# A gated four-branch decoder layer on one core: seven-product halves for 19 groups of column blocks in place of 7, with weight tiles placed by the form of the product

## Chip, cores and metric

The kernel runs on one core of a Trainium2 chip. The metric is the device time of one execution in microseconds (us). Every time below is from a run or from the profiled execution of the kernel before.

## What is computed

One layer, 256 tokens of width 2048, and 256 memory tokens, all in float32:

```python
xn = rms_norm(x, ln_g)
(a_q, a_k, a_v, a_g, c_b, c_c, c_h, c_g, s_q, s_k, s_v, s_g, m_q, m_g,      # 14 sections of 1024 columns
 i_q, i_k, i_w,                                                             # 324 columns of an indexer
 r_a, r_c, r_s, r_m) = [xn @ w for w in cols]                               # 4 gates of 2048 columns
y_a = moba_attention(a_q, a_k, a_v) * silu(a_g)                             # one block of 256: causal
y_c = c_b * short_conv(c_c * c_h, conv_w, conv_b) * silu(c_g)               # depthwise, width 3
y_s = dsa_attention(s_q, s_k, s_v, i_q, i_k, i_w) * silu(s_g)               # top 64 keys of each token
mk, mv = split(rms_norm(mem, mem_ln_g) @ w_mem_kv)
y_m = memory_attention(m_q, mk, mv) * silu(m_g)
merged = (sigmoid(r_a) * (y_a @ w_branch[0]) + sigmoid(r_c) * (y_c @ w_branch[1])
          + sigmoid(r_s) * (y_s @ w_branch[2]) + sigmoid(r_m) * (y_m @ w_branch[3]))
out = rms_norm(x + merged @ w_out, final_g)
```

## The kernel before

**Split products.** Each float32 operand is split into a high part (rounded by ScalarE, line 104) and a low part (the rest, by VectorE, line 105), and a product is three matmuls: high by high, high by low, low by high. Weights come from HBM in tiles `raw` of 1 MB (four buffers), and each is split in two steps of 128x1024 into `hi` and `lo` (four buffers each). So every weight costs ScalarE a cast and VectorE a subtraction beside TensorE's matmuls.

**Two forms.** In the form with tokens moving (`project_t`, `products_t`, lines 135 to 151) the weight block is stationary and 256 token columns move; the result stands with channels on partitions, as the attention wants it. A section of 1024 columns is 384 matmuls of 256 columns. In the form with weights moving (`project`, `products`, lines 157 to 177) a block of 128 tokens is stationary and 512 weight columns move; the result has tokens on partitions. Two blocks of 512 columns are 192 matmuls of 512 columns, which streams as many columns as the other form does.

**Seven-product halves.** `by_halves` (lines 222 to 270) takes two blocks of 512 columns, "a group" below. On the first 1024 rows of the weights it forms a two by two product (two blocks of tokens, two quarters of 512 rows, two column blocks) with seven products in place of eight; the other 1024 rows go through in plain form (`plain`). A group is 180 matmuls of 512 columns in place of 192. For it, sums of blocks of the activations are made once (`sums_of`, into `x_sums`), and sums of weight quarters each time: four subtractions of 128x2048 in place in `raw` (lines 241, 245, 251, 261). The quarters `b11`, `b12` and `b22` hold three of the four `raw` buffers for most of the group. The products pass through the banks `m`, `z`, `r`, `x`, `y`, and eight additions of 128x512 put them together (lines 248 to 269). Where weights are plain, VectorE makes 16 splits for two blocks; in a group it makes 22, since the products use sums as well.

**Where which form stands.** Token-moving: the sections for q, k and gates (`to_heads`, `to_gate`), the convolution's four, the indexer, and the memory's k. Weights moving and plain: the memory's v, the first of two halves (j = 0) of the gate columns of M, S and A, the branch projections `w` and the output. By halves: the v sections of S and A, the second gate halves of M, S and A, and both gate halves of C, seven groups. `finish` (line 584) makes the SiLU gate, then for each j the gate columns and `merge`, which multiplies the branch projection `w` by the gate and adds it up.

**Order.** The order of each engine's queue is made by a scheduler from the program's order and its own estimates; each engine then works its queue in that order. TensorE runs M, S, A and C in turn, with the attention's small matmuls set between the matmuls of the next projection.

Of the kernel before, what the change touches and what calls it, by code (L numbers as in the profile page):

```python
# [36 lines left out]
SECTIONS_T = [(c, W) for c in (M_Q, M_G, S_Q, S_K, S_G, A_Q, A_K, A_G, C_C, C_H, C_B, C_G)]  # L37
SECTIONS_N = [(S_V, W), (A_V, W), (R_0, 4 * D)]
# [6 lines left out]
TOPK = 64  # L45


@with_exitstack
def hybrid_kernel(ctx, tc, x, xT, mem, memT, ln_g, mem_ln_g, w_t, w_n, w_idx, conv_w, conv_b, w_mem_k, w_mem_v,
# [26 lines left out]
    cb = const.tile([P, 8], F32, name="cb")  # L76
    nc.gpsimd.dma_start(out=g_x, in_=ln_g)
# [255 lines left out]

    def to_gate(c0, val):

        y = big.tile([P, 8, 2, T], F32R, name="y", tag="y")
        for b in range(4):
            cs = slice(2 * b, 2 * b + 2)
            yt = tmp.tile([P, 2, T], F32, name="yt", tag="yt")
            copy_t(yt, project_t(w_t[FIRST[c0] + b], x_act), func=AF.Silu)  # L340
            nc.vector.tensor_mul(yt, yt, val[:, cs])
            split(y[:, cs, 0], y[:, cs, 1], yt)
# [161 lines left out]
    def first_columns(dst):  # L504
# [4 lines left out]
        for k0 in range(0, KC, 4):  # L509
            raw = raw_tile(NB).rearrange("p k (b c) -> p k b c", b=2)  # L510
            n = 1 if k0 == 0 else 2
            for k in range(k0, k0 + 4, n):
# [3 lines left out]
                for i in range(n):  # L516
                    if (k + i) % 2 == 0:
                        hi, lo = parts_tiles(NB, NB)
# [65 lines left out]
    def finish(b, gate, val, halved, after=None):  # L584

        y = to_gate(gate, val)
        for j in range(2):
            merge(b, j, gate_columns(b, j, halved[j]), y, after)

    finish(BR_M, M_G, q, (False, True))  # L590
# [7 lines left out]
    finish(BR_S, S_G, q, (False, True))  # L598
# [22 lines left out]
    for b in range(4):  # L621
        acc = project_t(w_t[FIRST[C_B] + b], x_act)
        for j in range(2):
            nc.vector.tensor_mul(cc[:, 2 * b + j], acc[j], cc[:, 2 * b + j])
# [11 lines left out]
    finish(BR_C, C_G, cc, (True, True), after=parts_of)  # L636
# [4 lines left out]
    junk = big.tile([P, 2, NB], F32, name="junk", tag="nat")  # L641
# [9 lines left out]
    for n, (c0, c) in enumerate(blocks):  # L651
        ns = slice(c0, c0 + c)
        acc = project(w_out[c0 // NB][:, :, c0 % NB:c0 % NB + c], lambda k: mt[:, k], "o", t_outer=(n == last))
        for t in range(2):
            o = xr[t][:, ns]
            nc.vector.tensor_add(o, acc[t], o)
            nc.scalar.activation(out=junk[:, t, :c], in_=o, func=AF.Square, accum_out=ss[:, t, n:n + 1])
            if n < last:
                nc.vector.tensor_mul(o, o, fg[:, ns])
            if n == last - 1:  # L660
                nc.vector.tensor_reduce(out=pre[:, t:t + 1], in_=ss[:, t, :last], axis=AX.X, op=ALU.add)
                nc.vector.tensor_scalar(pre[:, t:t + 1], pre[:, t:t + 1], 1.0 / D, EPS, op0=ALU.mult, op1=ALU.add)
            if n == last:
# [50 lines left out]
```

## Time and profile before

| | |
|---|---|
| three runs | 1397.42, 1400.25 (median), 1401.28 us |
| the profiled execution | 1398.06 us; span of its profile 1396.3 us |
| TensorE matmuls, weight loads | 99% and 89% of the span busy, 8796 of each |
| VectorE, ScalarE, GpSimd | 67%, 52%, 1% |
| mean DMA rate | 193 GB/s |

TensorE's matmuls are pipelined: the mean of one in the profile (some 390 ns for 512 columns) is longer than the distance from one start to the next. The distance is found from a stretch that holds one kind alone: its length and one duration more, over the count, since the count takes in what lies partly in the stretch. On VectorE too an instruction overlaps the next by some 80 ns, so a row of several is shorter than the sum of its durations.

### The profile page before, as it was taken

What the parts mean: (1) busy time and instruction counts of PE and PEld (TensorE: products, weight loads), DVE (VectorE), ACT (ScalarE), POOL (GpSimd) and SP (SyncE); (2) the same over time, 40 slices, a digit from 0 to 9 for tenths busy, and PEclk for the clock granted to TensorE, in tenths of its full rate; (3) what the DMA queues carried; (4) which work ended last, traced back from release to release, by engine and by line L of the source; (5) the groups of instructions that cost most, each with busy time, mean ns of one, the idle gap of its engine ahead of it and who ended that gap; (6) DMA issues with size and microseconds to landing.
All of it is one profiled execution on the core that took longest, in us unless ns stands there. A gap on an engine that the chain in (4) does not pass through costs nothing.

```text
span 1396.3 us, 21263 instructions
## 1 busy us (share of the span) xinstructions
PE 1380.4 (99%) x8796; PEld 1243.9 (89%) x8796; DVE 933.4 (67%) x1123; ACT 729.2 (52%) x991; POOL 11.0 (1%) x25
## 2 busy tenths in 40 slices
PE   9999999999999999999999999999999999999997
PEld 9998998789998898878999899878999998878887
DVE  7687764774848884596546885487547558787654
ACT  7663675453445684354445585445343345545443
POOL 1000000000000000000000000000000000000000
PEclk9999999999999999999999999999999999999999
DMA  9774545375554735537553746537555654736551
GB/s 343 291 271 173 191 156 180 128 266 189 172 197 133 254 128 183 189 135 247 188 193 133 243 150 211 182 125 266 183 181 187 225 192 148 265 130 241 183 197 73
DMA packets 49969, 269.49 MB, mean 193 GB/s; under 512 B 6656, under 2 KB 17456, under 8 KB 19024
## 3 DMA queue, kind: packets, MB, share of 16 engines
q1 hardware_dynamic: 48960, 264.03, 55.0%
q0 software_dynamic: 624, 3.31, 0.6%
q8 instruction: 69, 1.13, 0.3%
q10 hardware_dynamic: 288, 0.79, 0.1%
q14 instruction: 28, 0.23, 0.0%
HBM read 265.88 MB, written 2.10 MB: 192 GB/s over the span
## 4 chain that ended last, share of the span: by engine, by line
PE 85%; DVE 8%; DMA 3%; issue 2%; ACT 2%; SPq 0%; POOLq 0%; POOL 0%; DVEq 0%; ACTq 0%
PE acc L138 13%; PE acc L140 13%; PE acc L139 13%; DVE lo L105 5%; PE w L160 4%; PE w L161 4%; PE w L159 4%; PE r L159 4%; PE r L161 4%; PE r L160 4%; PE o L160 2%; PE o L161 2%; PE o L159 2%; DMA raw<-in_w_n 1%; PE y L160 1%
## 5 line engine op out<-in xcount | busy, mean ns | idle before, releaser
L105 DVE TENSOR_TENSOR lo<-raw,hi 128x1024 fp32r<-128x1024 f32 (+1 forms) x538 | 640.0, 1202 | 416.5 <-ACT hi L104 414.4
L104 ACT CAST hi<-raw 128x1024 fp32r<-128x1024 f32 (+1 forms) x538 | 552.2, 1032 | 547.8 <-PE acc L139 196.4
L139 PE MATMUL acc<-x_hl,hi 128*128 128x256 f32 x1520 | 426.0, 280 | 0.0
L138 PE MATMUL acc<-x_hl,hi 128*128 128x256 f32 x1520 | 425.4, 280 | 0.5 <-ACT qt L155 0.5
L140 PE MATMUL acc<-x_hl,lo 128*128 128x256 f32 x1520 | 425.8, 280 | 0.0
L140 PEld LDWEIGHTS acc<-x_hl,lo 128*128 128x128 f32 x1520 | 288.1, 190 | 0.1
L138 PEld LDWEIGHTS acc<-x_hl,hi 128*128 128x128 f32 x1520 | 284.8, 187 | 0.9 <-ACT qt L155 0.7
L139 PEld LDWEIGHTS acc<-x_hl,hi 128*128 128x128 f32 x1520 | 284.8, 187 | 0.2
L159 PE MATMUL w<-hi,y 128*128 128x512 f32 x256 | 99.9, 390 | 0.0
L161 PE MATMUL w<-hi,y 128*128 128x512 f32 x256 | 99.7, 389 | 0.0
L160 PE MATMUL w<-lo,y 128*128 128x512 f32 x256 | 99.6, 389 | 0.0
L159 PE MATMUL r<-hi,x_hl 128*128 128x512 f32 x248 | 98.3, 396 | 0.0
L161 PE MATMUL r<-hi,x_hl 128*128 128x512 f32 x248 | 97.9, 395 | 0.0
L160 PE MATMUL r<-lo,x_hl 128*128 128x512 f32 x248 | 97.6, 394 | 0.0
L159 PEld LDWEIGHTS w<-hi,y 128*128 128x128 f32 x256 | 48.1, 188 | 10.0
L161 PEld LDWEIGHTS w<-hi,y 128*128 128x128 f32 x256 | 48.1, 188 | 10.0
L160 PEld LDWEIGHTS w<-lo,y 128*128 128x128 f32 x256 | 48.1, 188 | 9.9
L161 PEld LDWEIGHTS r<-hi,x_hl 128*128 128x128 f32 x248 | 46.7, 188 | 10.6
L160 PEld LDWEIGHTS r<-lo,x_hl 128*128 128x128 f32 x248 | 46.7, 188 | 10.4
L159 PEld LDWEIGHTS r<-hi,x_hl 128*128 128x128 f32 x248 | 46.9, 189 | 10.2
L161 PE MATMUL o<-hi,mt 128*128 128x512 f32 (+1 forms) x160 | 55.3, 347 | 0.0
L160 PE MATMUL o<-lo,mt 128*128 128x512 f32 (+1 forms) x160 | 55.1, 346 | 0.0
(246 smaller groups left out, 1860.7 us busy)
## 6 DMA issues: line engine op xcount, KB each, us to landing
raw<-in_w_t SPq DMA_DIRECT2D x92, 1024.0 KB, 5.0
raw<-in_w_n SPq DMA_DIRECT2D x80, 1024.0 KB, 4.9
raw<-in_w_branch SPq DMA_DIRECT2D x32, 1024.0 KB, 5.3
raw<-in_w_out SPq DMA_DIRECT2D x16, 1024.0 KB, 4.8
raw<-in_w_mem_k SPq DMA_DIRECT2D x8, 1024.0 KB, 6.4
raw<-in_w_mem_v SPq DMA_DIRECT2D x8, 1024.0 KB, 5.5
raw<-in_w_t SPq DMA_DIRECT2D x16, 256.0 KB, 5.9
raw<-in_memT SPq DMA_DIRECT2D x2, 1024.0 KB, 8.8
```

Of the source, the lines that this page charges most:

```text
L104: nc.scalar.copy(out=hi, in_=src)
L105: nc.vector.tensor_sub(out=lo, in0=src, in1=hi.bitcast(F32))
L138: nc.tensor.matmul(o, lhsT=hi, rhs=a[:, 0], start=(k == 0), stop=False)
L139: nc.tensor.matmul(o, lhsT=hi, rhs=a[:, 1], start=False, stop=False)
L140: nc.tensor.matmul(o, lhsT=lo, rhs=a[:, 0], start=False, stop=(k == nk - 1))
L159: nc.tensor.matmul(o, lhsT=ah, rhs=hi, start=start, stop=False)
L160: nc.tensor.matmul(o, lhsT=ah, rhs=lo, start=False, stop=False)
L161: nc.tensor.matmul(o, lhsT=al, rhs=hi, start=False, stop=stop)
```

## The change

1. **Halves for twelve more groups.** The sections for q and k of S and A and the four of the convolution go from the token-moving form to groups of halves (eight groups); the first gate halves of M, S and A go from plain to halves (three); the first two blocks of the output go by halves, with sums of the merged activations, `m_sums` (one). 19 groups in all.
2. **Transposes.** q and k come out with tokens on partitions, so `transposed` turns them with 16 transposes of 128x128 on TensorE for a section, in four banks that ScalarE copies. In the convolution the products `c_c * c_h` and `silu(c_g) * c_b` are formed with tokens on partitions (`times`: four multiplications of 128x512 on VectorE) and each is turned once: six times 16 transposes. The convolution itself, 24 operations of 128x256 on VectorE, is as before, and now stands beside the group for `c_g`.
3. **Placement.** A `fill` of 224 bytes, `hi` and `lo` tiles of 2\*512+64 columns and a wider `u` set where tiles start. Before, `x_hl`, `mt` and the sums start 32 bytes past a multiple of 128, and `y`, `hi`, `lo` and `part` 96 bytes past one: in the weights-moving form `x_hl` and `hi` are 64 bytes apart, `y` and `hi` 0. After, all start at multiples of 128, but for `hi` and `lo` where 256-column weight blocks are used, which start 64 bytes past one (`place`): weights moving is 0 apart for `x_hl`, `mt`, the sums and `y`, tokens moving 64 apart, as before.
4. `yt` has one buffer in place of two; `junk` stands in the buffer of `y`.

The TensorE instructions go from 8796 to 7212: the matmuls of 512 columns from 3084 to 4476, those of 256 columns in split form from 5520 to 2448, the transposes from 102 to 198.

```diff
-SECTIONS_T = [(c, W) for c in (M_Q, M_G, S_Q, S_K, S_G, A_Q, A_K, A_G, C_C, C_H, C_B, C_G)]
-SECTIONS_N = [(S_V, W), (A_V, W), (R_0, 4 * D)]
+SECTIONS_T = [(c, W) for c in (M_Q, M_G, S_G, A_G)]
+SECTIONS_N = [(c, W) for c in (S_Q, S_K, S_V, A_Q, A_K, A_V, C_C, C_H, C_G, C_B)] + [(R_0, 4 * D)]
+STATIONARY = 64
+    fill = const.tile([P, 56], F32, name="fill")
...
+    def parts_tiles(w=NB, c=NB, place=0):
+        i = place // 4
+        return [spl.tile([P, 2 * NB + 64], F32R, name=n, tag=n)[:, i:i + 2 * NB]
+                .rearrange("p (k c) -> p k c", c=w)[:, :, :c] for n in ("hi", "lo")]
...
-                hi, lo = parts_tiles(w, c)
+                hi, lo = parts_tiles(w, c, STATIONARY if w == TB else 0)
...
+    def times(nat, dst):
+        def done(t, n, src, psum):
+            nc.vector.tensor_mul(part(dst, t, n), src, part(dst, t, n))
+        return done
+    def transposed(nat, done):
+        for c in range(0, 8, 2):
+            pp = halves(bank("tp", "s"))
+            for i in range(2):
+                for t in range(2):
+                    nc.tensor.transpose(pp[:, i, t * P:(t + 1) * P], nat[:, t, (c + i) * P:(c + i + 1) * P], ident)
+            done(c, pp)
     def to_heads(name, c0):
         dst = big.tile([P, 8, T], F32, name=name, tag=name)
-        for b in range(4):
-            copy_t(dst[:, 2 * b:2 * b + 2], project_t(w_t[FIRST[c0] + b], x_act))
+        nat = nat_tile("n" + name)
+        columns(c0, nat, kept(nat), True)
+        transposed(nat, lambda c, pp: nc.scalar.copy(out=dst[:, c:c + 2], in_=pp))
...
+    def finish(b, y, after=None, last=None):
         for j in range(2):
-            merge(b, j, gate_columns(b, j, halved[j]), y, after)
+            sig = gate_columns(b, j, True)
+            if j == 1 and last is not None:
+                last()
+            merge(b, j, sig, y, after)
...
-    cc = to_heads("qt", C_C)
+    uu = nat_tile("uu", "vv")
+    columns(C_C, uu, kept(uu), True)
+    nat = nat_tile("ch")
+    columns(C_H, nat, times(nat, uu), True)
...
+    transposed(uu, lambda c, pp: nc.scalar.copy(out=u[:, c:c + 2, 2:], in_=pp))
...
+    bg = nat_tile("bg", "vv")
+    columns(C_G, bg, through(bg, AF.Silu), True)
+    nat = nat_tile("cb")
+    columns(C_B, nat, times(nat, bg), True)
+    y = y_parts()
+    transposed(bg, lambda c, pp: gate_parts(y, yt_tile(), pp, cc, c))
...
+    finish(BR_C, y, after=parts_of, last=merged_sums)
+    sums_of(lambda k0, n: mt[:, k0:k0 + n], m_sums[0])
...
+        by_halves([w_out[0], w_out[1]], lambda k: mt[:, k], m_sums[0], nat,
+                  lambda t, n, src, psum: got.append((n, t, src)))
```

How the engines' queues change at three places. First TensorE at the seam between q and k of branch A (k begins here). Before, in the token-moving form, with `acc` the result, `x_hl` moving and `hi` or `lo` stationary:

```order
L138 MATMUL acc_6864<-x_hl_113,hi_6868 128x256
L139 MATMUL acc_6864<-x_hl_113,hi_6868 128x256
L140 MATMUL acc_6864<-x_hl_113,lo_6869 128x256
L138 MATMUL acc_6865<-x_hl_113,hi_6868 128x256
L139 MATMUL acc_6865<-x_hl_113,hi_6868 128x256
L140 MATMUL acc_6865<-x_hl_113,lo_6869 128x256
L138 MATMUL acc_6864<-x_hl_113,hi_6868 128x256
```

After, the end of the first product `m` of k's group, then q's transposes `tp`, then the plain part `z`:

```order
L166 MATMUL m<-hi,x_hl 128x512
L167 MATMUL m<-lo,x_hl 128x512
L168 MATMUL m<-hi,x_hl 128x512
L340 MATMUL tp<-ident,nqt 128x128 x2
L166 MATMUL z<-hi,x_hl 128x512
L167 MATMUL z<-lo,x_hl 128x512
L168 MATMUL z<-hi,x_hl 128x512
```

Behind the first product of 12 matmuls stand the first two transposes of q; `z` stands behind them. Next VectorE where the convolution stands (`u` its input, `cw` its weights, `lo<-raw,hi` the split of the next weights). Before, its operations for two column blocks stand between the splits of a token-moving section:

```order
L614 TENSOR_TENSOR u<-acc,qt 128x256 x2
L617 TENSOR_SCALAR qt<-u,cw,cb 128x256 x2
L619 SCALAR_TENSOR_TENSOR qt<-u,cw,qt 128x256
L105 TENSOR_TENSOR lo<-raw,hi 128x1024
L619 SCALAR_TENSOR_TENSOR qt<-u,cw,qt 128x256 x3
L105 TENSOR_TENSOR lo<-raw,hi 128x1024 x3
L614 TENSOR_TENSOR u<-acc,qt 128x256 x2
L617 TENSOR_SCALAR qt<-u,cw,cb 128x256 x2
L619 SCALAR_TENSOR_TENSOR qt<-u,cw,qt 128x256
```

After, in the group for `c_g`, with `cc` the convolution's result:

```order
L653 SCALAR_TENSOR_TENSOR cc<-u,cw,cc 128x256 x2
L110 TENSOR_TENSOR lo<-raw,hi 128x1024 x2
L653 SCALAR_TENSOR_TENSOR cc<-u,cw,cc 128x256
L651 TENSOR_SCALAR cc<-u,cw,cb 128x256
L653 SCALAR_TENSOR_TENSOR cc<-u,cw,cc 128x256
L651 TENSOR_SCALAR cc<-u,cw,cb 128x256 x5
L653 SCALAR_TENSOR_TENSOR cc<-u,cw,cc 128x256 x9
L268 TENSOR_TENSOR raw<-raw 128x2048
L653 SCALAR_TENSOR_TENSOR cc<-u,cw,cc 128x256
L110 TENSOR_TENSOR lo<-raw,hi 128x1024
L653 SCALAR_TENSOR_TENSOR cc<-u,cw,cc 128x256 x2
L110 TENSOR_TENSOR lo<-raw,hi 128x1024
```

18 operations of the convolution and a subtraction of weight quarters now stand between one split and the next. Last, VectorE in S's q section after the change, where the indexer's top-k (`MAX`, `MATCH_REPLACE` on `score`) stands between the group's own instructions:

```order
L110 TENSOR_TENSOR lo<-raw,hi 128x1024
L500 MAX m_3393<-score 128x8
L256 TENSOR_TENSOR nqt<-m,nqt 128x512
L110 TENSOR_TENSOR lo<-raw,hi 128x1024
L501 MATCH_REPLACE score<-m_3393,score 128x128
L268 TENSOR_TENSOR raw<-raw 128x2048
L110 TENSOR_TENSOR lo<-raw,hi 128x1024
L500 MAX m_3393<-score 128x8
L261 TENSOR_TENSOR nqt<-m,nqt 128x512
L262 TENSOR_TENSOR nqt<-m,nqt 128x512
```

Before, these rounds stood between the splits of the token-moving q section, with no `raw<-raw` and no `nqt` among them.

## Rows read from the trace of the kernel before

**Rows 1.** The page of the kernel before, its first part (busy time, share of the span, instructions), and from its fourth part (the chain of work that ended last) the line by engine.

```profile
PE 1380.4 (99%) x8796; PEld 1243.9 (89%) x8796; DVE 933.4 (67%) x1123; ACT 729.2 (52%) x991; POOL 11.0 (1%) x25
PE 85%; DVE 8%; DMA 3%; issue 2%; ACT 2%; SPq 0%; POOLq 0%; POOL 0%; DVEq 0%; ACTq 0%
```

**Rows 2.** Busy time by stretch (the windows view). Columns: the stretch in us and its length; for each engine its busy time and, in brackets, the instructions that lie at least partly in it; the granted share of the clock; the DMA engines' share; GB/s. In order: the q, k and v sections of branch S; S's earlier gate half; the k section of branch A; A's later gate half; the two gate halves of branch C; the first two column blocks of the output.

```profile
342.70:389.40 46.70, 46.70 (x405) 46.49 (x404) 36.08 (x79) 20.99 (x29) 1.10 (x2) 1.00 0.58 197
389.40:432.90 43.50, 43.50 (x387) 43.50 (x386) 21.75 (x18) 19.34 (x26) 0.00 (x0) 1.00 0.52 180
432.90:476.00 43.10, 42.88 (x194) 35.02 (x193) 38.29 (x40) 26.52 (x32) 0.00 (x0) 1.00 0.60 208
531.90:576.70 44.80, 44.80 (x195) 36.29 (x194) 20.83 (x18) 20.49 (x23) 0.00 (x0) 1.00 0.55 182
710.60:755.80 45.20, 45.20 (x386) 45.20 (x385) 21.93 (x18) 19.25 (x26) 0.00 (x0) 1.00 0.50 171
921.40:965.30 43.90, 42.27 (x182) 33.50 (x181) 38.80 (x37) 23.99 (x25) 0.00 (x0) 1.00 0.59 203
1168.00:1210.40 42.40, 42.06 (x183) 33.47 (x182) 37.33 (x35) 26.08 (x29) 0.53 (x1) 1.00 0.67 236
1233.10:1276.40 43.30, 42.36 (x182) 33.40 (x181) 38.14 (x36) 23.98 (x25) 0.00 (x0) 1.00 0.60 208
1299.90:1344.80 44.90, 44.90 (x202) 36.90 (x202) 25.61 (x27) 19.14 (x22) 0.00 (x0) 1.00 0.51 178
```

**Rows 3.** The same view inside stretches that hold one kind of product alone: `acc` of S's q and k sections; `acc` of the convolution's sections; `r` of S's earlier gate half; `w` of branch A; `r` of M's earlier gate half.

```profile
360.00:430.00 70.00, 70.00 (x620) 70.00 (x619) 44.38 (x78) 30.54 (x39) 0.00 (x0) 1.00 0.57 195
990.00:1160.00 170.00, 170.00 (x1446) 170.00 (x1445) 91.72 (x106) 69.47 (x78) 0.54 (x1) 1.00 0.56 192
534.00:574.00 40.00, 40.00 (x173) 32.42 (x172) 18.69 (x17) 17.49 (x18) 0.00 (x0) 1.00 0.55 185
901.00:921.00 20.00, 20.00 (x90) 16.58 (x89) 13.40 (x13) 7.73 (x8) 0.00 (x0) 1.00 0.46 157
221.00:237.00 16.00, 16.00 (x71) 13.13 (x70) 7.53 (x7) 5.88 (x7) 0.00 (x0) 1.00 0.60 198
```

**Rows 4.** VectorE's instructions in the later gate half of branch A, 921.4 to 965.3 us, grouped by line and shape (busy us, mean ns of one | idle before, and on what).

```profile
L105 DVE TENSOR_TENSOR lo<-raw,hi 128x1024 fp32r<-128x1024 f32 x23 | 27.2, 1219 | 4.8 <-ACT hi L104 4.8
L245 DVE TENSOR_TENSOR raw<-raw 128x2048 f32<-128x2048 f32 x1 | 2.3, 2284 | 0.0
L248 DVE TENSOR_TENSOR sig<-m,sig 128x512 f32<-128x512 f32 x1 | 0.7, 684 | 0.0
```

**Rows 5.** VectorE's timeline in the same stretch: start, length of the row, line, operands, count, and idle time before it with what ended it.

```profile
942.84 2.29 DVE L261 TENSOR_TENSOR raw<-raw 128x2048 f32<-128x2048 f32 x1 [0.29 <-DMA raw<-in_w_n]
946.18 0.68 DVE L254 TENSOR_TENSOR sig<-m,sig 128x512 f32<-128x512 f32 x1
946.78 0.68 DVE L255 TENSOR_TENSOR sig<-m,sig 128x512 f32<-128x512 f32 x1
951.98 5.76 DVE L105 TENSOR_TENSOR lo<-raw,hi 128x1024 fp32r<-128x1024 f32 x5
```

**Rows 6.** The chain that ended last, followed through the same stretch (start us, us, what).

```profile
929.92 2.21 DVE raw L245
932.24 1.05 ACT hi L104
933.31 0.98 DVE lo L105
934.46 3.50 DVE lo L105 x3
937.97 4.84 DMA raw<-in_w_n
942.84 1.21 DVE raw L261
...
953.25 0.50 PE y L160
```

**Rows 7.** All waits of TensorE (the waits view): who waited for whom, us in total, times, longest; its rows on `m` and `y`.

```profile
PE m L160 <- DVE lo L105: 3.3, 5, 0.8
PE m L159 <- ACT hi L104: 1.6, 2, 0.8
PE y L160 <- DVE lo L105: 0.4, 2, 0.2
```

**Rows 8.** TensorE's timeline where branch C's merged columns are transposed: the eight transposes, and the product behind them.

```profile
1227.41 1.04 PE L633 MATMUL pp<-ident,merged 128*128 128x128 f32 x8
1228.21 0.48 PE L159 MATMUL w<-hi,y 128*128 128x512 f32 x1
```

**Rows 9.** VectorE's groups, by line and shape: the convolution's operations on its eight column blocks (two lines); the indexer's top-k, its eight rounds on the full width, in S's q section (two lines); the split of one sum of the activations.

```profile
L617 DVE TENSOR_SCALAR qt<-u,cw,cb 128x256 f32<-128x256 f32 x8 | 2.9, 406 | 0.0
L619 DVE SCALAR_TENSOR_TENSOR qt<-u,cw,qt 128x256 f32<-128x256 f32 x16 | 7.0, 478 | 0.0
L469 DVE MAX8 m<-score 128x8 f32<-128x256 f32 x8 | 3.4, 426 | 0.2
L470 DVE MATCH_REPLACE8 score<-m,score 128x256 f32<-128x256 f32 x8 | 3.3, 409 | 0.0
L105 DVE TENSOR_TENSOR x_sums<-g,x_sums 128x512 fp32r<-128x512 f32 x4 | 2.6, 683 | 0.0
```

More of the change, by code (lines that the diff above doesn't have):

```diff
@@ L517, in first_columns @@
                     if (k + i) % 2 == 0:
[L518 removed]
+                        hi, lo = parts_tiles(place=STATIONARY)
                     split_tokens(xraw[:, k + i], k + i, g_x, x_hl[:, k + i])
@@ L620, in hybrid_kernel @@
                                            op0=ALU.mult, op1=ALU.add)
[L621 to L624, printed above, removed]
+    bg = nat_tile("bg", "vv")
+    columns(C_G, bg, through(bg, AF.Silu), True)
+    nat = nat_tile("cb")
+    columns(C_B, nat, times(nat, bg), True)
+    y = y_parts()
+    transposed(bg, lambda c, pp: gate_parts(y, yt_tile(), pp, cc, c))
     mt = big.tile([P, KC, 2, T], F32R, name="mt", tag="xhl")
@@ L650, in hybrid_kernel @@
     inv = const.tile([P, 2], F32, name="o_inv")
-    for n, (c0, c) in enumerate(blocks):
-        ns = slice(c0, c0 + c)
[L653 to L663, printed above, removed]
-                nc.vector.tensor_scalar(var[:, t:t + 1], ss[:, t, n:], 1.0 / D, pre[:, t:t + 1], op0=ALU.mult,
-                                        op1=ALU.add)
-                nc.gpsimd.tensor_tensor(out=inv[:, t:t + 1], in0=var[:, t:t + 1], in1=mhalf[:, 0:1], op=ALU.pow)
-                nc.vector.tensor_mul(o, o, fg[:, ns])
-                for eng, cs in ((nc.vector, slice(0, 512)), (nc.scalar, slice(512, 1280)), (nc.vector, slice(1280, D))):
-                    o = xr[t][:, cs]
-                    if eng is nc.vector:
-                        nc.vector.tensor_scalar(o, o, inv[:, t:t + 1], None, op0=ALU.mult)
-                    else:
-                        nc.scalar.activation(out=o, in_=o, func=AF.Copy, scale=inv[:, t:t + 1])
-                    (nc.scalar if eng is nc.scalar else nc.sync).dma_start(out=out[t * P:(t + 1) * P, cs], in_=o)
@@ new lines, in blocks_of @@
+    def blocks_of():
+        got = []
+        nat = nat_tile("no")
+        by_halves([w_out[0], w_out[1]], lambda k: mt[:, k], m_sums[0], nat,
+                  lambda t, n, src, psum: got.append((n, t, src)))
+        yield from got
+        for n, (c0, c) in enumerate(blocks[2:], 2):
+            acc = project(w_out[c0 // NB][:, :, c0 % NB:c0 % NB + c], lambda k: mt[:, k], "o", t_outer=(n == last))
+            yield from ((n, t, acc[t]) for t in range(2))
+    for n, t, src in blocks_of():
+        c0, c = blocks[n]
+        ns = slice(c0, c0 + c)
+        o = xr[t][:, ns]
+        nc.vector.tensor_add(o, src, o)
+        nc.scalar.activation(out=junk[:, t, :c], in_=o, func=AF.Square, accum_out=ss[:, t, n:n + 1])
+        if n < last:
+            nc.vector.tensor_mul(o, o, fg[:, ns])
+        if n == last - 1:
+            nc.vector.tensor_reduce(out=pre[:, t:t + 1], in_=ss[:, t, :last], axis=AX.X, op=ALU.add)
+            nc.vector.tensor_scalar(pre[:, t:t + 1], pre[:, t:t + 1], 1.0 / D, EPS, op0=ALU.mult, op1=ALU.add)
+        if n == last:
+            nc.vector.tensor_scalar(var[:, t:t + 1], ss[:, t, n:], 1.0 / D, pre[:, t:t + 1], op0=ALU.mult,
+                                    op1=ALU.add)
+            nc.gpsimd.tensor_tensor(out=inv[:, t:t + 1], in0=var[:, t:t + 1], in1=mhalf[:, 0:1], op=ALU.pow)
+            nc.vector.tensor_mul(o, o, fg[:, ns])
+            for eng, cs in ((nc.vector, slice(0, 512)), (nc.scalar, slice(512, 1280)), (nc.vector, slice(1280, D))):
+                o = xr[t][:, cs]
+                if eng is nc.vector:
+                    nc.vector.tensor_scalar(o, o, inv[:, t:t + 1], None, op0=ALU.mult)
+                else:
+                    nc.scalar.activation(out=o, in_=o, func=AF.Copy, scale=inv[:, t:t + 1])
+                (nc.scalar if eng is nc.scalar else nc.sync).dma_start(out=out[t * P:(t + 1) * P, cs], in_=o)
```

39 lines of the change are left out of this document (19 added, 20 removed).

## The prediction

> **What bounds the kernel now.** I read the page first: TensorE is busy for 99% of the span and holds 85% of the chain that ended last, VectorE is busy for 67% [rows 1]. So I priced stretches by what TensorE streams, and looked in each for the engine that could take over.
>
> The stretches [rows 2] show two kinds. Where weights are plain, TensorE is busy all the time and VectorE half of it: 21.75 of 43.5 us in k of S, 21.9 of 45.2 in k of A, 20.8 of 44.8 in S's earlier gate half. In a group of halves VectorE is busy for 37.3 to 38.8 us of 42.4 to 43.9, and TensorE shows its only gaps. So the change trades the bound that is met everywhere (streamed columns) for work on an engine that is nearly full in just these groups.
>
> The pace [rows 3] (length and one duration, over the count) is not one number for one form. Token-moving matmuls of 256 columns start every 113.4 ns in one stretch (70.28 us over 620) and 117.8 ns in another (170.28 over 1446). Weight-moving ones of 512 columns start every 226.5 ns on `y` (20.39 over 90), 231 on `x_hl` in M's gate half (16.39 over 71) and 233.5 on `x_hl` in S's (40.39 over 173). The granted clock is full in all. What differs between the first and the last two of these is where the tiles start: `y` is 0 bytes from `hi` modulo 128, `x_hl` 64. After the change all weight-moving matmuls have the start that `y` has, so I price all at 226.5 ns: a group is 180 x 226.5 ns = 40.8 us.
>
> **The change part by part.** All sums are made against the profiled execution's span, 1396.3 us.
>
> *Token-moving sections to halves.* q of S lasts 46.7 us, of which I leave 2.4 us to the indexer's small matmuls (384 at 115.4 ns are 44.3); k of S 43.5; the six others stand as k of A does, 45.2 each, 271.2 [rows 2]. Together 359.0 us; eight groups are 326.4. **-32.6.**
>
> *Plain halves and output to halves.* S's gate half 44.8, A's the same, M's 192 x 231 ns = 44.3, the two output blocks 44.9 less 0.8 for eight transposes = 44.1 [rows 2, 3]. Together 178.0; four groups are 163.2. **-14.8.**
>
> *Placement, for what stays in form.* The seven old groups lie between the paces 226.5 and 233.5 [rows 3]; I take 229, near the middle, so 180 x 2.5 ns = 0.45 us each, 3.2, and with the memory's v and the third output block (288 matmuls) 0.7 more: **-3.9**. The token-moving matmuls that are left (2064) stay 64 bytes apart, and I leave them at 0; whether they go into the 113.4 or the 117.8 state is open, and the whole difference is 2064 x 4.4 ns = 9.1 us, of which I give the range -5 to +4.
>
> Against this stands a rule. The Trainium skill, "SBUF — State Buffer", section "Who interferes with whom", says "PE and ACT never wait on anyone", and its table of paths gives the weight load a second, independent read port; by it no placement matters. This trace does not agree: 226.5 against 233.5 ns for the same shape at the same clock. By the rule the placement's terms are nothing, and the sum is that of the third rival.
>
> *Transposes.* Eight take 0.80 us, from 1227.41 to 1228.21 [rows 8], and they stand in TensorE's queue, so all of it counts: 96 x 0.1 = **+9.6**. ScalarE's copies of them, 24 of 128x512, replace 64 copies of accumulators and are hidden, ScalarE being busy 24 to 26 us of a group [rows 2].
>
> *Waits inside a group.* A group is 22 splits, four subtractions of 128x2048 and eight additions of 128x512 on VectorE [rows 4] (one of the 23 splits there is the neighbour's). In a row a split takes 5.76/5 = 1.15 us; a subtraction 2.2 and an addition 0.6 from one start to the next [rows 5, 6]. That is 25.3 + 8.8 + 4.8 = 38.9 us, beside 40.8 us of matmuls. So VectorE keeps up, with 5% to spare, if it never waits. The existing groups last 42.4 to 43.9 us [rows 2] where 180 x 229 ns are 41.2: 1.2 to 2.7 over, when they follow `w`, whose merges VectorE still has to do. S's v follows a token-moving section and lasts 43.1, of which 14 of its 194 matmuls and their edges, about 1.4 us, are attention's: some 0.5 over. The gaps are waits of `m` for splits, 0.8 us at most [rows 7]. I take 0.8 for the three gate halves, which follow token-moving sections, and 1.3 for the nine others: **+14.1**. The bounds are 0.3 and, if nothing overlapped the landing of the fourth quarter, 38.9 + 4.84 [rows 6] + two casts of 1.05 = 45.8 us, 5.0 over.
>
> *VectorE's other work that loses its cover.* The convolution's 24 operations are 9.9 us busy [rows 9], less the overlap of 80 ns each about 8.0. Before they lay in plain sections with 20 us to spare. Now 18 of them and a subtraction stand between two splits, some 6.2 + 2.2 us in which TensorE has no more than the splits already made: four buffers, a pair of which lasts 1.4 us in a product and 2.7 in the plain part. So 5 to 11 us are covered; I take +4 of a possible 0 to 8. The top-k, 6.7 us on the full width [rows 9] and somewhat less on half of it, falls on q and k of S: +2, of 0 to 8. The gate's four products and splits in C's first gate half: +1.5. The sums of the merged activations take four splits of 0.68 [rows 9], six more operations about as long, and two of the four `raw` buffers: +2.5, of 0 to 6. **+10.** The rest costs nothing: `yt` with one buffer is used once in four steps of 11 us, and the four multiplications of `times` are 2.4 us each in C's c_h and c_b, inside their 1.3.
>
> Sum: -32.6 - 14.8 - 3.9 + 9.6 + 14.1 + 10 = **-17.6 us**, a span of 1378.7. The profiled execution took 1398.06, 1.8 more than its span and 2.2 under the median of the runs, which lie within 3.9 us. From the execution I come to 1380.5, from the median to 1382.7, and I say 1382.
>
> **The rivals.**
>
> *TensorE alone decides* (lower). The scheduler hides what VectorE adds: waits of 0.5 in each of the twelve groups and no more, 6 in place of 24.1. That is -35.7, 1364.5 from the median. For it: S's v, with attention's work in it, is only 0.5 over. Against it: rows 6, where the chain runs through VectorE and a DMA for 23 us of an existing group.
>
> *VectorE and the raw buffers set the groups* (slower). Eleven groups stand back to back or nearly so: S's q, k, v, A's q, k, v, the convolution's four, C's first gate. In each the fourth quarter `b21` waits for a `raw` buffer, lands after 4.84 us, is subtracted and split [rows 6]. If VectorE has nothing else to do meanwhile, a group lasts 45.8 us; my sum has about 42.3 for it, so 11 x 3.5 = 38 more, +21, 1421. It decides from 17.6/11 = 1.6 us a group on. Against it: in the existing group VectorE idled only 0.29 us for that landing [rows 5], since other splits stood in its queue.
>
> *The placement does nothing* (same side, small). All groups stay at 229 ns: 12 x 0.45 and the 3.9 are lost, -8.3, 1392.
>
> *The placement is harmful* (slower, the change doesn't do what it says). If the slow state of `r` is not a matter of distance and all 19 groups run at 233.5 ns, 3420 x 7 ns = 24 us are lost, +6, 1407. Against it: every `w` stretch that I looked at has 226.5.
>
> *Starts at multiples of 64 make matmuls faster still.* All split tiles start 32 bytes past a multiple of 64 now, and none does after, so no row shows this case. If it gave one more step like that from 233.5 to 226.5 ns, 4476 matmuls would give back 31 us, 1351; VectorE's 38.9 us a group would then bind at once. The Trainium skill, "TensorE: Matmul & The Clock Gate", section "Back-to-back issue gap", gives N/2.4 + 2.5 ns, 215.8 for 512 columns, by which it would be 48 us; no stretch here comes under 226.
>
> **How the numbers follow.** A measurement of this kernel tells about 0.3%, 4 us, from no change. My forecast, with its bounds on waits and states from 1371 to 1394, has 0.56; TensorE alone 0.18; VectorE and buffers 0.09; no placement 0.10; harmful placement 0.04; faster still 0.03. The range 1362 to 1397 takes in the first two and the fourth and leaves out the two slower ones, the fastest, and a little of the forecast's edges, some 0.2. Faster by over 0.3%: 0.54 of the 0.56, 0.18, 0.03, and 0.07 of the fourth, 0.82. Slower: the 0.13 of the two but for 0.04 in which they are mild, 0.09. Within: 0.09.
>
> **What would show it.** In the profile after: stretches of halves on `x_hl` at 226 to 227 ns a matmul; groups of 42 to 43 us, with gaps of TensorE on `m` behind splits; VectorE above 80% of the span and 90% in the back-to-back groups; the group of `c_g` some 4 us longer than that of `c_b`, with its gap behind the convolution; q and k of S longer than those of A. I am wrong if groups back to back last over 44 us, if the pace on `x_hl` isn't that on `y`, or if TensorE waits for DMA itself.

## The result, and the profile after

The changed kernel takes 1417.61 us (median of four runs, 1415.59 to 1418.57), the kernel before 1399.15 us beside it (1397.42 to 1401.28): 1.0129 times as long, 95% interval 1.0110 to 1.0149. The profiled execution took 1417.77 us with a span of 1416.0 us, against 1398.06 and 1396.3. I had forecast 1382 with a range to 1397; the time is outside of it and on the other side. Two executions in the series below, one of the kernel before (2645.08 us) and one of the kernel with both another order and half-size subtractions (1495.38 us), ran at mean granted clocks of 0.52 and 0.85 and are left out of every comparison.

The page of the changed kernel, where [rows 1] were read: busy times, and the chain that ended last by engine.

```profile
PE 1372.2 (97%) x7212; PEld 1161.2 (82%) x7212; DVE 1169.7 (83%) x1341; ACT 805.1 (57%) x1055; POOL 11.2 (1%) x26
...
PE 62%; DVE 25%; issue 5%; ACT 4%; DMA 3%; SPq 0%; DVEq 0%; POOLq 0%; POOL 0%; ACTq 0%
```

TensorE is busy for less time than before (1372.2 us in place of 1380.4), and part of that is not work: some waits do not show as gaps, and some matmuls run at half clock. The same matmuls are busy for 1340.2 us in a kernel without subtractions, which comes below. The chain that sets the end now runs through VectorE for 25% in place of 8%. Where TensorE waits is in the waits view (who waited for whom, us in total, times, longest), to be read against [rows 7]:

```profile
PE m L167 <- DVE lo L110: 8.8, 13, 0.8
PE m L166 <- ACT hi L109: 8.5, 6, 2.9
PE m L166 <- DVE bg L255: 4.2, 1, 4.2
```

By stretch (columns as in [rows 2]): q, k and v of S; S's earlier gate half; k of A; the convolution's c_c and c_g; C's earlier gate half; the output's first two blocks.

```profile
348.10:394.50 46.40, 45.01 (x200) 36.01 (x199) 46.14 (x66) 24.96 (x28) 1.10 (x2) 1.00 0.52 184
394.50:441.30 46.80, 44.42 (x198) 34.92 (x197) 46.11 (x65) 25.31 (x28) 0.00 (x0) 1.00 0.51 180
441.30:486.70 45.40, 44.94 (x209) 36.41 (x208) 40.28 (x43) 27.98 (x35) 0.00 (x0) 1.00 0.57 194
542.70:584.50 41.80, 41.71 (x182) 33.46 (x181) 36.79 (x34) 26.16 (x29) 0.00 (x0) 1.00 0.62 215
717.60:761.80 44.20, 43.45 (x198) 35.08 (x197) 39.20 (x36) 25.34 (x28) 0.00 (x0) 1.00 0.54 191
993.30:1038.10 44.80, 42.50 (x181) 33.40 (x180) 40.35 (x37) 23.18 (x23) 0.00 (x0) 1.00 0.54 188
1081.40:1136.40 55.00, 47.96 (x197) 38.10 (x196) 49.25 (x61) 27.40 (x30) 0.57 (x1) 0.91 0.47 172
1179.60:1226.10 46.50, 44.44 (x197) 34.87 (x196) 43.13 (x45) 27.23 (x30) 1.07 (x2) 1.00 0.63 227
1315.20:1364.40 49.20, 45.81 (x191) 36.57 (x190) 45.05 (x44) 25.55 (x29) 0.00 (x0) 0.93 0.58 204
```

Against [rows 2]: S's q 46.7 before, 46.4 now; k 43.5, 46.8; v 43.1, 45.4 though its form did not change; S's gate half 44.8, 41.8; k of A 45.2, 44.2; C's gate half 42.4, 46.5; the output 44.9, 49.2. The section c_g, token-moving and 45.2 us before, takes 55.0. Only groups behind a token-moving section are clearly shorter. VectorE is busy for 39 to 49 us of each of the longer ones, and TensorE shows gaps in all of them. The largest loss next to c_g is M's earlier gate half, in which memory attention's VectorE work stands too, 48.2 us before and 53.3 after:

```profile
191.30:239.50 48.20, 48.20 (x230) 40.24 (x229) 25.77 (x30) 27.37 (x37) 0.53 (x1) 1.00 0.52 171
```
```profile
191.60:244.90 53.30, 48.57 (x218) 39.49 (x217) 42.46 (x47) 33.89 (x43) 0.53 (x1) 0.94 0.49 168
```

What such a gap is made of stands in the timeline of c_c's group (start us, us, what; in brackets the idle time before it and what ended it): VectorE's rows, then ScalarE's, then TensorE's where it waited.

```profile
1001.87 2.29 DVE L252 TENSOR_TENSOR raw<-raw 128x2048 f32<-128x2048 f32 x1
1005.35 3.50 DVE L110 TENSOR_TENSOR lo<-raw,hi 128x1024 fp32r<-128x1024 f32 x3 [1.19 <-ACT hi L109]
...
1004.27 3.90 ACT L109 CAST hi<-raw 128x1024 fp32r<-128x1024 f32 x4 [6.52 <-DVE raw L252]
...
1005.37 0.50 PE L166 MATMUL m<-hi,x_sums 128*128 128x512 f32 x1 [1.03 <-ACT hi L109]
1006.63 0.50 PE L167 MATMUL m<-lo,x_sums 128*128 128x512 f32 x1 [0.76 <-DVE lo L110]
```

Three engines take turns. From 1001.87 VectorE subtracts one weight block from another (2.29 us); ScalarE has been idle for 6.52 us and can cast the difference only when all of it is there, at 1004.27; VectorE idles for 1.19 us until the first cast is done, at 1005.35; TensorE, which has used up its split tiles, waits 1.03 us for the cast and 0.76 us for the split. By the starts of its matmuls, 2.3 of the group's 4.0 us over 40.8 are lost in this product, and most of the rest at single splits later on, of which those for `z` and `y` are of blocks as loaded; they stand in the same queue of VectorE.

### The profile page after: what moved, and what is told of

Read it like the earlier page. It is cut to its first block, busy times and chain, and to the rows that moved or that the text cites. A ratio compares the mean times of both kernels' runs of the same rounds, so it can differ in the third digit from the quotient of the medians.

```text
span 1416.0 us, 18418 instructions
## 1 busy us (share of the span) xinstructions
PE 1372.2 (97%) x7212; PEld 1161.2 (82%) x7212; DVE 1169.7 (83%) x1341; ACT 805.1 (57%) x1055; POOL 11.2 (1%) x26
## 3 DMA queue, kind: packets, MB, share of 16 engines
q1 hardware_dynamic: 48960, 264.03, 53.3%
## 4 chain that ended last, share of the span: by engine, by line
PE 62%; DVE 25%; issue 5%; ACT 4%; DMA 3%; SPq 0%; DVEq 0%; POOLq 0%; POOL 0%; ACTq 0%
DVE lo L110 14%; PE acc L145 4%; PE acc L146 4%; PE acc L147 4%; PE y L167 4%; PE y L168 3%; PE w L168 3%; PE w L167 3%; PE w L166 3%; PE y L166 3%; PE x L168 3%; PE x L167 3%; DMA raw<-in_w_n 3%; PE x L166 3%; ACT hi L109 2%
## 5 line engine op out<-in xcount | busy, mean ns | idle before, releaser
L146 PE MATMUL acc<-x_hl,hi 128*128 128x256 f32 (+1 forms) x496 | 139.8, 282 | 0.0
L147 PE MATMUL acc<-x_hl,lo 128*128 128x256 f32 (+1 forms) x496 | 139.6, 282 | 0.0
L145 PE MATMUL acc<-x_hl,hi 128*128 128x256 f32 (+1 forms) x496 | 138.9, 280 | 0.0
L166 PE MATMUL m<-hi,x_sums 128*128 128x512 f32 x216 | 87.7, 406 | 9.9 <-ACT hi L109 5.6
L167 PE MATMUL m<-lo,x_sums 128*128 128x512 f32 x216 | 88.6, 410 | 8.3 <-DVE lo L110 8.3
L146 PEld LDWEIGHTS acc<-x_hl,hi 128*128 128x128 f32 (+1 forms) x496 | 92.9, 187 | 0.1
L145 PEld LDWEIGHTS acc<-x_hl,hi 128*128 128x128 f32 (+1 forms) x496 | 92.8, 187 | 0.1
L147 PEld LDWEIGHTS acc<-x_hl,lo 128*128 128x128 f32 (+1 forms) x496 | 92.7, 187 | 0.0
L167 PE MATMUL y<-lo,x_hl 128*128 128x512 f32 x216 | 87.3, 404 | 3.6 <-DVE lo L110 2.5
L167 PE MATMUL x<-lo,x_hl 128*128 128x512 f32 x216 | 85.6, 396 | 0.9 <-DVE lo L110 0.8
L166 PE MATMUL x<-hi,x_hl 128*128 128x512 f32 x216 | 85.2, 394 | 1.2 <-ACT hi L109 1.0
L168 PE MATMUL m<-hi,x_sums 128*128 128x512 f32 x216 | 86.2, 399 | 0.0
L166 PE MATMUL y<-hi,x_hl 128*128 128x512 f32 x216 | 84.9, 393 | 0.8 <-ACT hi L109 0.7
L168 PE MATMUL y<-hi,x_hl 128*128 128x512 f32 x216 | 84.4, 391 | 0.0
L168 PE MATMUL x<-hi,x_hl 128*128 128x512 f32 x216 | 84.3, 390 | 0.0
L166 PEld LDWEIGHTS m<-hi,x_sums 128*128 128x128 f32 x216 | 41.7, 193 | 22.2 <-ACT hi L109 9.1
```

The lines of the kernel that those rows point to most:

```text
L145: nc.tensor.matmul(o, lhsT=hi, rhs=a[:, 0], start=(k == 0), stop=False)
L146: nc.tensor.matmul(o, lhsT=hi, rhs=a[:, 1], start=False, stop=False)
L147: nc.tensor.matmul(o, lhsT=lo, rhs=a[:, 0], start=False, stop=(k == nk - 1))
L166: nc.tensor.matmul(o, lhsT=ah, rhs=hi, start=start, stop=False)
L167: nc.tensor.matmul(o, lhsT=ah, rhs=lo, start=False, stop=False)
L168: nc.tensor.matmul(o, lhsT=al, rhs=hi, start=False, stop=stop)
```

## The experiments

My theories after the result. **A:** the subtractions of weight blocks on VectorE set the groups, either by VectorE's amount of work (A1) or because a split has to wait for its subtraction (A2). **B:** TensorE and its clock set them. **C:** the new placement does harm. And the rival of the prediction, that the raw buffers and the landing of the fourth quarter do it.

**The layout alone.** The kernel before with `fill`, the places of `hi` and `lo`, the wider `u` and one `yt`:

```diff
+    fill = const.tile([P, 56], F32, name="fill")
...
-                hi, lo = parts_tiles(w, c)
+                hi, lo = parts_tiles(w, c, STATIONARY if w == TB else 0)
...
```

> The kernel before with the changed layout alone (fill, form-dependent starts of hi and lo, wider u, one yt buffer); every section keeps the form that it had before. Theory A, halves are set by VectorE and the buffers: the plain weight-moving stretches go from 233.5 and 231 to 226.5 ns a matmul, 1.0 to 1.3 us for each of the three gate halves and the two output blocks; the seven old groups give 0 to 0.5 us each; together 6 to 10 us, 1390 to 1394. Theory C, the placement was what made the change slow: 1400 or above. The token-moving sections may come out in the 113.4 or the 117.8 ns pace, which moves either figure by up to 10 us.

Measured: 1395.53 us, 0.998 of the kernel before (0.9969 to 0.9990). The placement is not what made the change slow (C falls), and it gives a little less than A expected: the old groups of halves stay nearly as they were, S's later gate half at 44.9 us (45.1 before), though their matmuls now start 227 ns apart in the median in place of 229 to 231. The plain stretch of S's earlier gate half, which [rows 3] has with 173 matmuls, now holds 178 in the same 40 us, 226.9 ns each:

```profile
534.00:574.00 40.00, 40.00 (x178) 33.13 (x177) 19.16 (x17) 18.21 (x19) 0.00 (x0) 1.00 0.55 185
```

**The change with the old layout.**

```diff
-    fill = const.tile([P, 56], F32, name="fill")
...
-STATIONARY = 64
+STATIONARY = 0
...
-    u = big.tile([P, 8 * (T + 16)], F32, name="u", tag="kt")[:, :8 * (T + 2)].rearrange("p (c t) -> p c t", c=8)
+    u = big.tile([P, 8, T + 2], F32, name="u", tag="kt")
```

> The changed kernel with the layout of before: hi and lo 64 bytes from x_hl again (modulo 128). Theory A, VectorE and the buffers set the groups that stand back to back: TensorE's slower pace goes into its waits, 0 to 6 us in all, 1418 to 1424. Theory of the prediction, TensorE sets the groups: 3420 matmuls on x_hl and the sums by 2.5 to 7 ns are 8.6 to 24 us, 1426 to 1441. Theory C, the placement is harmful: below 1415.

Measured: 1418.47 us, 1.0134 of the kernel before (1.0114 to 1.0155), 0.9 us above the changed kernel: the 3420 matmuls of the groups start 230 to 231 ns apart in the median in place of 227, some 12 us in all if each counted, and cost nothing that can be told. TensorE's pace does not set these groups.

**Without the subtractions.**

```diff
-        nc.vector.tensor_sub(out=b11, in0=b12, in1=b11)
-        product(m5, s(0), b11, True, True)
+        product(m5, s(0), b12, True, True)
...
```

> The changed kernel without the four subtractions of weight blocks in each group: the products take the weights as loaded, so the output is another one; matmuls, splits and loads are all still there. Theory A, VectorE sets the groups: 19 groups lose 8.8 us of VectorE each, groups back to back come to 41 to 42.5 us, the half-clock stretches behind waits mostly go, and the time is 1365 to 1385. Theory B, the groups are as long as TensorE and a falling clock make them, and VectorE's part is hidden: 1405 to 1417, and some 30 us at half clock as before.

Measured: 1354.30 us, one run, and no half clock ahead of the last microseconds. That is 63.3 us less than the changed kernel, more than A expected, and B falls. The 19 groups (from the first matmul into `m` to the last into `x` or `y`, shared stretches counted once) go from 867.2 to 804.2 us, so all of it comes from them.

**The subtractions made, but not waited for.** The four lines stay; the products take `b12`, `b22` and `b21` as loaded.

```diff
         nc.vector.tensor_sub(out=b11, in0=b12, in1=b11)
         m5 = bank("m", tag)
-        product(m5, s(0), b11, True, True)
+        product(m5, s(0), b12, True, True)
...
```

> The changed kernel with the four subtractions still made, in place and at their turn, but read by no split: the products take the weights as loaded, so the output is another one. VectorE has the same work and the buffers live as long; what is gone is that a split must wait for its subtraction. Theory A1, VectorE's amount of work sets a group: groups back to back stay at 44 to 45 us, 1405 to 1418. Theory A2, the wait for the subtraction sets it (subtraction 2.2, cast 1.05, split 1.15 in a row, with only four pairs of split tiles ahead): groups fall to 41 to 42 us, 1355 to 1380.

Measured: 1380.80 us, one run, 0.8 above A2's range and far below A1's; the groups take 827.3 us. So of the 63.3 us, 36.8 go when no split has to wait for its subtraction, and 26.5 stay with the subtractions' work and the buffers that they hold (the two weren't separated).

**Half-size subtractions.** The same arithmetic, in two instructions:

```diff
+    def less(out, b, a):
+
+        for h in (0, 2):
+            nc.vector.tensor_sub(out=out[:, h:h + 2], in0=b[:, h:h + 2], in1=a[:, h:h + 2])
...
-        nc.vector.tensor_sub(out=b11, in0=b12, in1=b11)
+        less(b11, b12, b11)
```

> The changed kernel with each subtraction of 128x2048 made as two of 128x1024, so that the first cast can start 1.1 us earlier and the cast runs beside the second subtraction; some 0.1 us more VectorE work for each. Theory A1 (amount of work): no change or up to 6 us slower, 1416 to 1424. Theory A2 (the row of waits): 76 subtractions give back up to 1.1 us each where TensorE waits, 10 to 50 us, 1365 to 1408.

Measured: 1390.39 us, 0.9939 of the kernel before (0.9924 to 0.9953): 27 us less than the changed kernel, the groups at 839.2 us, while VectorE is busy for slightly longer (1173.9 us against 1169.7). A2 holds, A1 falls. One half-clock stretch of 6.8 us is left of six, so a part of the gain may come with the clock; but q of A and c_c, which had no such stretch, fall by 2.9 and 3.1 us too. The timeline at the same place, VectorE's rows and ScalarE's:

```profile
983.25 2.35 DVE L232 TENSOR_TENSOR raw<-raw 128x1024 f32<-128x1024 f32 x2
985.66 4.63 DVE L110 TENSOR_TENSOR lo<-raw,hi 128x1024 fp32r<-128x1024 f32 x4
...
984.57 5.05 ACT L109 CAST hi<-raw 128x1024 fp32r<-128x1024 f32 x5 [4.41 <-DVE raw L232]
```

ScalarE starts its cast at 984.57, while the second of the two subtractions still runs, and VectorE goes from its two subtractions to the split with no idle time shown. Shorter instructions also let the scheduler set other work between the two, here a split and a step of branch A's merge:

```profile
974.03 1.22 DVE L232 TENSOR_TENSOR raw<-raw 128x1024 f32<-128x1024 f32 x1
975.17 1.22 DVE L110 TENSOR_TENSOR lo<-raw,hi 128x1024 fp32r<-128x1024 f32 x1
976.30 0.68 DVE L534 TENSOR_TENSOR sig<-w,sig 128x512 f32<-128x512 f32 x1
976.90 1.22 DVE L232 TENSOR_TENSOR raw<-raw 128x1024 f32<-128x1024 f32 x1
```

How much of the 27 us comes from the earlier cast and how much from this finer order, no run separates; that the wait for a subtraction counts by itself is shown by the run ahead of this one.

c_c's group by the windows view, one row from each of four kernels: without subtractions; subtractions not waited for; half-size; and three pairs of split tiles, which comes next.

```profile
961.00:1001.80 40.80, 40.80 (x182) 33.79 (x181) 32.05 (x33) 23.70 (x23) 0.00 (x0) 1.00 0.58 205
```
```profile
974.20:1016.30 42.10, 41.66 (x181) 33.51 (x180) 40.01 (x37) 23.49 (x23) 0.00 (x0) 1.00 0.55 200
```
```profile
975.70:1017.40 41.70, 41.38 (x181) 33.63 (x180) 40.02 (x40) 23.38 (x23) 0.00 (x0) 1.00 0.55 202
```
```profile
1039.00:1088.40 49.40, 43.49 (x182) 33.23 (x182) 40.74 (x37) 23.45 (x23) 0.00 (x0) 1.00 0.48 169
```

40.8 us is 180 x 226.5 ns, no wait at all. VectorE is busy for 40.35, 40.01 and 40.02 us in the changed kernel, the one that does not wait and the one with half-size subtractions; the groups last 44.8, 42.1 and 41.7 us. Equal work, other order.

**Three pairs of split tiles** in place of four.

```diff
-    spl = ctx.enter_context(tc.tile_pool(name="spl", bufs=4))
+    spl = ctx.enter_context(tc.tile_pool(name="spl", bufs=3))
```

> The changed kernel with three pairs of split tiles in place of four; same work and same loads. Theory A2 (the row subtraction, cast, split is bridged only by the splits that are made ahead): one split less ahead is up to 1.4 us more for each of the 76 subtracted products, 1435 to 1500. Theory of the raw buffers (the fourth quarter's landing sets a group): the wait for a load is the same, 1416 to 1425.

Measured: 1497.38 us, one run, 79.8 us more, with the same loads; the groups take 944.1 us, 76.9 more. Over the 76 subtracted products that is 1.0 us each, within the 1.4 expected, and the theory of the raw buffers, 1416 to 1425, falls. So the groups depend on how many splits are made ahead; three pairs without subtractions were not run, so it isn't shown that all of it belongs to the subtracted products.

**Another order of steps.**

```diff
-        m7 = bank("m", tag)
+        m7 = bank("m7", "pp")
         product(m7, s(2), b12, True, True)
+        x, y = bank("x", tag), bank("y", tag)
+        plain((y, x), act, srcs[0], 8, (True, True), (False, False))
...
```

> The changed kernel with a group's steps in another order: the third plain quarter is worked between m7 and the product of z (m7 in a bank of its own), so that no more than two products with a subtracted block follow each other without plain work, in which TensorE takes 5.4 us for two splits. Same work on every engine. Theory A1: groups are bound by VectorE's sum and stay, 1410 to 1420. Theory A2: VectorE's late products find split tiles ahead, 1 to 2 us a group less, 1380 to 1400. A loss is possible where a load comes later for want of a raw buffer, up to 1425.

Measured: 1412.11 us, 1.0091 (1.0069 to 1.0112), 5.5 us less than the changed kernel, inside what A1 expected and short of A2. More plain work between the products helps little here; why is open. With half-size subtractions as well:

> Both of the last two edits. Theory A1: 1412 to 1424. Theory A2: the gains add in part, 1355 to 1395, and the kernel is faster than the one before.

Measured: 1387.58 us, the median of three runs, 0.9915 (0.9882 to 0.9949), not told apart from the half-size subtractions alone.

**Without the work beside.** The convolution's 24 operations and the top-k's 16 pairs are left out.

```diff
-            for _ in range(TOPK // 8):
-                nc.vector.max(out=m8, in_=score[:, cs])
-                nc.vector.match_replace(out=score[:, cs], in_to_replace=m8, in_values=score[:, cs], imm_value=TAKEN)
...
-    cc = big.tile([P, 8, T], F32, name="cc", tag="qt")
-    for c in range(8):
...
+    cc = u[:, :, 2:]
```

> The changed kernel without the convolution's 24 operations (the gate takes u as it is) and without the 16 pairs of the top-k. Theory A with the lost cover: the group of c_g falls from 55.0 to 44 to 46 us and its two half-clock stretches go, q and k of S fall by 1 to 2 us each, 1402 to 1406. Theory B: the group of c_g stays above 50, since the clock falls for other reasons, 1411 to 1417. The other groups stay as they are in both.

Measured: 1406.08 us, one run, 11.5 us less. c_g's stage falls from 55.0 to 48.9 us, less than expected; q of S by 0.2 us and k by 2.6, to 44.2, A's length. How the convolution costs: VectorE's timeline of the changed kernel in c_g, and TensorE's wait.

```profile
1101.85 3.64 DVE L653 SCALAR_TENSOR_TENSOR cc<-u,cw,cc 128x256 f32<-128x256 f32 x9
1105.42 2.28 DVE L268 TENSOR_TENSOR raw<-raw 128x2048 f32<-128x2048 f32 x1
...
1109.15 0.87 DVE L653 SCALAR_TENSOR_TENSOR cc<-u,cw,cc 128x256 f32<-128x256 f32 x2
...
1111.08 0.68 DVE L255 TENSOR_TENSOR bg<-m,bg 128x512 f32<-128x512 f32 x1
...
1111.81 0.80 PE L166 MATMUL m<-hi,x_sums 128*128 128x512 f32 x1 [4.21 <-DVE bg L255]
```

The addition that empties a bank of `m` (1111.08) stands behind the convolution's operations, and TensorE waits 4.21 us for that bank. It is a bank that is late there, not a split. With half-size subtractions, where the same stage still lasts 53.3 us, its longest wait is for a split:

```profile
PE z L167 <- DVE lo L110: 5.4, 1, 5.4
```

So in both kernels the stage loses its time to something late on VectorE, once an addition and once a split.

**The half-size subtractions in the kernel before**, with the layout (the diffs of the first and the fifth experiment together):

> The kernel before with the changed layout and half-size subtractions in its seven groups of halves. Theory A2: the groups of 42.3 to 44.9 us come to 41 to 42, 6 to 14 us less than the 1395.5 of the layout alone, 1381 to 1390. Theory A1 (amount of VectorE work): as the layout alone, 1394 to 1397, since VectorE has a little more to do.

Measured: 1385.38 us, 0.9912 (0.9898 to 0.9927), as A2 expected.

**A mixed kernel**, from the one with half-size subtractions; the output is all `project` again:

```diff
+SECTIONS_T = [(c, W) for c in (M_Q, M_G, S_Q, S_G, A_G, C_G)]
...
+    gt = by_tokens(big.tile([P, 8, T], F32, name="gt", tag="vv"), C_G, AF.Silu)
+    nc.vector.tensor_mul(cc, cc, gt)
+    nat = nat_tile("cb")
+    columns(C_B, nat, kept(nat), True)
...
-            sig = gate_columns(b, j, True)
+            merge(b, j, gate_columns(b, j, first or j == 1), y, after)
...
+    finish(BR_M, to_gate(M_G, q), False)
...
+    finish(BR_C, y, False, parts_of)
```

> The changed kernel with half-size subtractions, and with the form of before for the sections that stand beside other VectorE work: q of S (top-k), c_g (convolution; its gate is multiplied into the convolution's result), the earlier gate halves of M (sums of the tokens) and C, and all of the output. Theory A2 with lost cover: from the 1390 of the half-size subtractions, c_g's stage falls from 53 to about 46, the first gate half of C by 2.5, the output by 3.5, M's first gate half by 1 to 4, k of S by 1 to 3; 1368 to 1378, 1.5 to 2.2% below the kernel before. If cover has nothing to do with it, these sections lose their shorter form and the time is 1390 to 1400.

Measured: 1377.32 us, 0.9853 of the kernel before (0.9839 to 0.9867), faster than both kernels. Its k of S and q of A in halves; c_g, token-moving beside the convolution; C's earlier gate half and the output's first two blocks, plain:

```profile
387.70:428.80 41.10, 41.05 (x182) 33.67 (x181) 37.58 (x36) 24.06 (x25) 0.00 (x0) 1.00 0.57 205
656.50:698.30 41.80, 41.36 (x182) 33.57 (x182) 39.52 (x40) 23.47 (x23) 0.00 (x0) 1.00 0.56 202
1055.00:1101.00 46.00, 46.00 (x392) 45.93 (x391) 32.88 (x47) 21.91 (x27) 0.57 (x1) 1.00 0.54 195
1143.70:1188.40 44.70, 44.70 (x206) 37.06 (x205) 25.11 (x25) 21.16 (x24) 0.53 (x1) 1.00 0.60 206
1275.80:1320.20 44.40, 44.40 (x202) 36.85 (x201) 25.49 (x27) 19.17 (x22) 0.00 (x0) 1.00 0.52 181
```

TensorE is busy for the whole of the last three; the groups are 41.1 and 41.8 us.

**The mixed kernel with whole subtractions.**

> The mixed kernel with each subtraction of 128x2048 whole again. If the row subtraction, cast, split costs what the runs so far say (27 us over 19 groups, 10 us over the seven of before), its 14 groups lose 15 to 22 us, 1392 to 1400, and the choice of sections alone brings little against the kernel before. If the choice of sections had been the cause, 1377 to 1382 stays.

Measured: 1395.28 us, 0.9979 (0.9967 to 0.9991): 18 of the 21 us that the mixed kernel gains hang on the size of the subtractions.

## Why the prediction was wrong

**What failed: the term for waits inside a group, +14.1.** I summed VectorE's 38.9 us against TensorE's 40.8 and wrote that VectorE keeps up "with 5% to spare, if it never waits". The sum was right: VectorE is busy for 40 us in c_c's group at any of its lengths from 41.7 to 44.8. But a product with a subtracted block lasts 12 x 226.5 ns = 2.7 us on TensorE, and its first split comes at the end of a row of three, subtraction 2.2, cast 1.05, split 1.15 us, which passes from VectorE to ScalarE and back. That row stood in [rows 6], the first three lines; I priced the transfer behind it and not the row. Four pairs of split tiles do not bridge it: the products wait for it, 36.8 us in all by the run that does not wait. The groups back to back, c_g's apart, took 43.2 to 46.8 us; c_c's, with only four steps of branch A's merge beside it, 4.0 over 40.8, not 1.3.

**The size of it.** My span without the two terms for waits (14.1 and 10) was 1354.6; with no subtractions the span is 1352.5. So pace, transposes and the count of groups were right together to 2 us, though errors may cancel in that sum. In place of the 24.1 us of these two terms the kernel pays 63.5 (1416.0 - 1352.5). With the subtractions not waited for, the span is 1379.0, near my 1378.7: I had priced the work and left out the row. That it is so near is luck in part, since M's earlier gate half (48.7 us there, 45.5 by my terms) and c_g's stage (50.6, 47.7) still lie above my sum and others below.

**Work that loses its cover, +10.** For c_g I took +4; leaving the convolution out gives 6.1. Its mechanism was a bank's release and not the splits that I had named. The top-k, +2, was about right: 2.8 in q and k of S together. The sums in front of the output and C's first gate half, +4, were too low: these stages stand at 49.2 and 46.5 us, where my terms give 45.4 and 45.1, and at 44.4 and 44.7 in plain form in the mixed kernel. And for M's earlier gate half I had no such term at all, though memory attention stands in it: 53.3 us, 7.8 over the 45.5 of my terms. It falls to 48.7 when no split waits for its subtraction; what attention's work costs of the rest no run separates.

**Pace and placement.** Right as a pace: 40.8 us for a group without waits is 226.5 ns a matmul on `x_hl` too. Wrong as a gain for the old groups: they hardly got shorter with it (1.0 us in all seven, where I had 3.2), nor the changed kernel's groups clearly longer without it. The third rival, a placement that does nothing, is true of groups of halves and not of the pace. The two paces, 226.5 here and 233.5 on the same tile in [rows 3], do not agree with what I had drawn from the Trainium skill ("SBUF — State Buffer", section "Who interferes with whom"), that no placement matters. The rule that I quoted from it is about engines that wait on each other, and no run here tests that.

**Transposes, +9.6.** Right: k of A without subtractions lasts 42.6 us, 1.8 over 40.8 for 16 transposes of its neighbour's columns, 0.11 each.

**The rivals.** The slower one, VectorE and the raw buffers, gave 45.8 us a group and 1421, and the sign, the group and the total came out nearly so. That was luck, since its mechanism, the fourth quarter's landing, is not what sets the groups: with the same loads and buffers, half-size subtractions bring c_c's group to 41.7 us, and the chain after has 3% for DMA, as before. It had 0.09; the row that I held against it, VectorE's idle time of 0.29 us for a landing [rows 5], says nothing of waits for a cast (4.8 us in the same stretch, [rows 4]). TensorE alone, 1364.5, is reached only once nothing is subtracted (1354.3).

**The clock** I had not priced. Behind waits of TensorE, or during one, the granted clock falls from 1.0 to 0.5, that is from 2.4 to 1.2 GHz: one stretch of 3.4 us before (612.6 to 616.0), six after, of 3.4 to 6.8 us, 30.7 in all. Two of them, 6.8 and 3.4 us:

```profile
1111.10:1117.90 6.80, 6.09 (x14) 4.84 (x15) 5.31 (x7) 1.60 (x2) 0.09 (x1) 0.50 0.88 334
619.50:622.90 3.40, 3.40 (x8) 2.73 (x9) 3.35 (x3) 2.39 (x3) 0.00 (x0) 0.51 0.01 2
```

In one group that waits for VectorE such a stretch adds little: q of A in the changed kernel without such a stretch, and in the mixed kernel with whole subtractions with one of 3.4 us (mean clock 0.96), last 44.7 and 44.8 us.

```profile
672.90:717.60 44.70, 42.55 (x182) 33.40 (x181) 40.31 (x37) 23.28 (x23) 0.00 (x0) 1.00 0.54 188
```
```profile
662.90:707.70 44.80, 43.13 (x181) 34.82 (x180) 40.49 (x37) 23.46 (x23) 0.00 (x0) 0.96 0.52 188
```

Where the wait is for a bank or for something outside, as in c_g, what the clock itself costs stays open; no run holds it up with the wait in place.

**Open besides:** how the 26.5 us of the subtractions that nobody waits for part into VectorE's work and held buffers; why the other order of steps gave only 5.5 us; how the 27 us of the half-size subtractions part into the earlier cast and the finer order of VectorE's queue.

## What to carry to other kernels

An engine that is busy for less than TensorE in a stage can still set it: write down, for the shortest product, the row of dependent steps across engines ahead of its first matmul, and compare that row, not the sum, with what the tiles made ahead can bridge. Cut an instruction that stands in such a row so that the next engine can start on its first part; with 76 casts that can start 1.1 us earlier, and an order with shorter instructions, that was worth 27 us here, at the same work. And use the form with fewer matmuls only where the side engine has nothing else queued ahead of what TensorE waits for, be it a split or the addition that empties a bank.

## What the hardware showed that I had not expected

Taking one of four pairs of split tiles away costs 79.8 us, four times the whole change: the kernel stands at a steep place in that number. A stretch of 3.4 us at half clock left q of A as long as it is without one (44.8 and 44.7 us), so the 30.7 us of such stretches cannot simply be added to a sum. And a matmul's pace that differs by nearly 2% with the tiles' starts (medians of 227 against 230 to 231 ns) moved the changed kernel by under 1 us, though it was some 12 us of matmuls.
